# A three-layer float32 block on one core: the order on the engines comes from the scheduler's other machine model

## The chip, the core and the metric

The kernel runs on one core of a Trainium2 chip. The core has engines that each work through a queue of their own, in the order in which the queue was filled: TensorE (PE, matrix products; its weight loads are shown apart as PEld), VectorE (DVE), ScalarE (ACT), GpSimd (POOL) and SyncE (SP, which here only starts transfers). An instruction whose inputs are not there holds everything behind it on its own engine. The metric is the device time of one execution in microseconds (us), lower is better; the median over runs counts.

## What is computed

The reference is two blocks, one after the other, in float32, on 512 tokens of width 1024. Cut to what matters here:

```
# first block: 16 meta tokens are put ahead of the 512
h = h + 0.5 * swiglu(rmsnorm(h, norm_ffn1), w_ffn1_in, w_ffn1_out)
u = rmsnorm(h, norm_mix)
...                                   # u @ w_in -> fox attention, 16 heads; retention, 4 heads
mixed = g_a * (y_a @ w_o_fox) + g_b * (y_b @ w_o_ret)
h = h + mixed @ w_out
h = h + 0.5 * swiglu(rmsnorm(h, norm_ffn2), w_ffn2_in, w_ffn2_out)

# second block, two layers; the first of them also carries 256 context tokens on
h = modulate(x, sh1, sc1)             # layer_norm(x) * (1 + scale) + shift
y = ...                               # neighbourhood attention, spatial gating, grouped-query attention, @ w_o
x = layer_norm(ALPHA * x + g1 * y) * ln1_g[l] + ln1_b[l]
x = layer_norm(ALPHA * x + g2 * swiglu_2(modulate(x, sh2, sc2), ...)) * ln2_g[l] + ln2_b[l]
```

## The kernel before, in words

Activations lie transposed: eight tiles of 128 channels, tokens along the free axis, worked on in two halves of 256, 272 or 384 tokens. A product with a weight matrix runs in units of 128 output channels. Each unit's weights come from HBM by a transfer on SP's queue (`raw`), ACT rounds them to the high part (`whi`, line 269), DVE or POOL takes the rest (`wlo`, line 271), and `mm3` issues three products for each of the eight channel tiles: high by high (line 300), low activation (line 301), low weight (line 303). With eight tiles a unit is 24 matmuls on each half of the tokens. Three `whi`/`wlo` pairs and three `raw` tiles are in rotation, so the split of a later unit waits until an earlier unit's matmuls are done.

Between products stand norms. A layer norm of one half (`ln`) is a chain over four engines, and `postln` followed by `modulate` is two such chains, one behind the other:

1. POOL adds the tiles in pairs (line 1157), PE takes the mean over channels of the sums by a product with a constant matrix (line 1163, four matmuls), which leaves the mean in a PSUM tile;
2. DVE subtracts the mean from each of eight tiles (line 1168), ACT squares (line 1169), POOL adds the squares (line 441);
3. PE sums the squares over channels with single-column products (line 369); DVE makes the reciprocal root in ten small steps (lines 376, 333 to 353) and a diagonal matrix of it, `dg` (line 394);
4. PE spreads `dg` over all partitions (line 407); `postln` then scales on DVE and shifts on ACT (lines 1205, 1206), `modulate` writes the activations of the next product, high part on ACT (`ah`, line 1194) and low part on DVE (`al`, lines 1191, 1195).

The program is written by generators: a phase's products are written out, and the norm of the other half is advanced a step at a time between units. Three PSUM pools hold the results: `mm` for units, `at` for statistics, means, spreads and some units.

`run` wraps the program in a manual schedule for POOL, so POOL's queue keeps the order in which the program is written. The queues of PE, DVE, ACT and SP are filled by the framework's scheduler. It reads the whole program, plays it on a model of the machine, and where several instructions could go next on an engine it places the one that the model has ready; the program's order decides among those ready. Which model plays is an argument of the tile context. `_trace` opens two contexts: a dry one, whose only product is the list of weight units, and the real one.

Of the kernel before, what the change touches and what calls it, by code (L numbers as in the profile page):

```python
# [2069 lines left out]
def _trace(nc, I, out):  # L2070

    import concourse.bacc as bacc

    dry = bacc.Bacc("TRN2", target_bir_lowering=False, num_devices=1)
    J = {k: dry.dram_tensor("in_" + k, v.shape, F32, kind="ExternalInput").ap() for k, v in I.items()}
    o = dry.dram_tensor("out", out.shape, F32, kind="ExternalOutput").ap()
    plan = None
    try:
        with tile.TileContext(dry) as tc, ExitStack() as ctx:
            k = Kern(ctx, tc, J, o)  # L2080
            k.run()
            plan = k.plan
            raise _Dry
    except _Dry:
        pass
    with tile.TileContext(nc) as tc, ExitStack() as ctx:
        Kern(ctx, tc, I, out, plan).run()


# [12 lines left out]
```

## Time and profile before

| | |
|---|---|
| runs | 3388.63, 3375.97, 3386.22 us; median 3386.22 |
| the profiled execution | 3384.84 us |
| its span | 3383.0 us, so 1.84 us lie around the span |
| PE busy | 3220.5 us, 95% of the span, 19680 matmuls |
| DVE busy | 2088.1 us, 62% |
| ACT busy | 1320.8 us, 39% |
| POOL busy | 531.9 us, 16% |
| mean granted clock of PE | 0.978 of full speed |

PE is the engine that is nearly always busy. What is not PE's work is the idle time before a PE instruction, and each view of the waits names the step that ended it. A granted clock of 1.00 is 2.4 GHz and of 0.50 is 1.2 GHz.

### The profile page before, as it was taken

Reading aid. Unit: us, or ns where it says so; the run is one execution under the profiler, and the core shown is the slowest. Engines: PE = TensorE matmul, PEld = TensorE weight load, DVE = VectorE, ACT = ScalarE, POOL = GpSimd, SP = SyncE. Lnnn points to the kernel's source line nnn. Section 1 sums busy time; section 2 is a strip of 40 time slices with the busy share of each in tenths; the row PEclk is TensorE's granted clock in tenths of the full one; section 3 lists DMA queues with packets and bytes.
Section 4 is the critical chain, followed back from the end, with each engine's and each line's share of the span. In section 5 each row is a group of like instructions: output and inputs, shape, how many; then the busy total and the mean of one; then the engine's idle time right before and its main releaser. Section 6 shows DMA issues by size and latency. Waiting matters only on the chain. (4 is left out here: it accounts for less than half of the span.)

```text
span 3383.0 us, 50315 instructions
## 1 busy us (share of the span) xinstructions
PE 3220.5 (95%) x19680; PEld 2874.1 (85%) x19680; DVE 2088.1 (62%) x4433; ACT 1320.8 (39%) x2266; POOL 531.9 (16%) x500
## 2 busy tenths in 40 slices
PE   8999999999999999999898989999999999889998
PEld 8999979988888987889777878888898787888887
DVE  7994568876633769856676764222257586773335
ACT  4222346653323523234464543111135365552223
POOL 2000122333200100012212240000013212320001
PEclk9999999999999999999999999999999799999999
DMA  6663431122233556644001322221234201333233
GB/s 209 209 206 103 124 97 45 51 68 69 65 96 101 194 175 196 211 122 143 19 28 53 92 75 90 65 65 57 69 117 137 74 24 57 118 125 112 88 98 107
DMA packets 112461, 351.22 MB, mean 104 GB/s; under 512 B 12960, under 2 KB 26912, under 8 KB 111968
## 3 DMA queue, kind: packets, MB, share of 16 engines
q1 hardware_dynamic: 86464, 280.07, 26.8%
q10 hardware_dynamic: 25472, 65.84, 6.1%
q8 instruction: 155, 2.54, 0.3%
q0 software_dynamic: 288, 2.10, 0.2%
q14 instruction: 82, 0.67, 0.1%
HBM read 339.57 MB, written 8.39 MB: 103 GB/s over the span
## 5 line engine op out<-in xcount | busy, mean ns | idle before, releaser
L269 ACT ACTIVATE whi<-raw 128x1024 fp32r<-128x1024 f32 (+3 forms) x543 | 549.3, 1012 | 1413.8 <-PE mm L301 757.3
L300 PE MATMUL mm<-ah,whi 128*128 128x512 f32 (+3 forms) x2496 | 811.4, 331 | 11.9 <-ACT s L576 5.4
L301 PE MATMUL mm<-al,whi 128*128 128x512 f32 (+3 forms) x2496 | 787.5, 327 | 1.0 <-DVE al L1195 1.0
L271 DVE TENSOR_TENSOR wlo<-raw,whi 128x1024 fp32r<-128x1024 f32 (+2 forms) x464 | 559.5, 1208 | 328.7 <-ACT whi L269 324.6
L303 PE MATMUL mm<-ah,wlo 128*128 128x512 f32 (+3 forms) x2496 | 717.1, 328 | 5.5 <-DVE wlo L271 5.5
L300 PEld LDWEIGHTS mm<-ah,whi 128*128 128x128 f32 x2496 | 476.1, 191 | 65.2 <-ACT ah L1194 7.4
L301 PEld LDWEIGHTS mm<-al,whi 128*128 128x128 f32 x2496 | 475.8, 191 | 41.4 <-DVE al L1195 3.3
L300 PE MATMUL at<-ah,whi 128*128 128x512 f32 (+4 forms) x1368 | 479.5, 352 | 8.3 <-DVE B L1482 2.6
L301 PE MATMUL at<-al,whi 128*128 128x512 f32 (+4 forms) x1368 | 459.5, 337 | 0.1
L303 PEld LDWEIGHTS mm<-ah,wlo 128*128 128x128 f32 x2496 | 430.4, 191 | 32.9 <-DVE wlo L271 6.5
L303 PE MATMUL at<-ah,wlo 128*128 128x512 f32 (+4 forms) x1368 | 457.6, 336 | 0.0
L300 PE MATMUL mm<-gh,whi 128*128 128x256 f32 (+3 forms) x1168 | 377.0, 327 | 0.7 <-ACT gh L322 0.3
L301 PE MATMUL mm<-gl,whi 128*128 128x256 f32 (+3 forms) x1168 | 366.8, 323 | 0.7 <-DVE gl L323 0.7
L303 PE MATMUL mm<-gh,wlo 128*128 128x256 f32 (+3 forms) x1168 | 339.3, 324 | 0.3 <-DVE wlo L271 0.3
L300 PEld LDWEIGHTS at<-ah,whi 128*128 128x128 f32 x1368 | 265.6, 195 | 34.0 <-issue 5.3
L301 PEld LDWEIGHTS at<-al,whi 128*128 128x128 f32 x1368 | 266.4, 195 | 23.6 <-issue 3.3
L303 PEld LDWEIGHTS at<-ah,wlo 128*128 128x128 f32 x1368 | 265.5, 194 | 21.3 <-issue 0.5
L1157 POOL TENSOR_TENSOR sq<-x,x 128x256 f32<-128x256 f32 (+1 forms) x68 | 73.2, 1088 | 1211.2 <-DVE x L1214 815.1
L300 PEld LDWEIGHTS mm<-gh,whi 128*128 128x128 f32 x1168 | 220.6, 189 | 23.1 <-ACT gh L322 0.5
L301 PEld LDWEIGHTS mm<-gl,whi 128*128 128x128 f32 x1168 | 220.8, 189 | 17.9 <-DVE gl L323 1.4
L271 POOL TENSOR_TENSOR wlo<-raw,whi 128x1024 fp32r<-128x1024 f32 (+1 forms) x79 | 181.5, 2305 | 316.4 <-ACT whi L269 316.2
L582 DVE TENSOR_TENSOR s<-s,mm 128x256 f32<-128x256 f32 (+3 forms) x142 | 71.9, 525 | 233.7 <-PE mm L303 232.8
(403 smaller groups left out, 4839.4 us busy)
## 6 DMA issues: line engine op xcount, KB each, us to landing
raw<-in_wfin SPq DMA_DIRECT2D x116, 512.0 KB, 3.5
raw<-in_win SPq DMA_DIRECT2D x115, 512.0 KB, 3.6
wm<-in_wmod ACTq DMA_DIRECT2D x96, 512.0 KB, 4.2
raw<-in_w2in SPq DMA_DIRECT2D x52, 512.0 KB, 4.4
raw<-in_w1in SPq DMA_DIRECT2D x50, 512.0 KB, 3.7
raw<-in_wfout SPq DMA_DIRECT2D x48, 448.0 KB, 3.3
raw<-in_w1out SPq DMA_DIRECT2D x24, 448.0 KB, 3.4
raw<-in_w2out SPq DMA_DIRECT2D x24, 448.0 KB, 3.3
```

The lines of the kernel that those rows point to most:

```text
L269: self.nc.scalar.activation(hi, raw, AF.Copy)
L271: eng.tensor_tensor(lo, raw, hi.bitcast(F32), op=ALU.subtract)
L300: t.matmul(ps, wh, xh, start=start, stop=False)
L301: t.matmul(ps, wh, xl, start=False, stop=False)
L303: t.matmul(ps, wl, xh, start=False, stop=stop)
L582: nc.vector.tensor_tensor(s[:, c], s[:, c], ps[1][:, 512 * b:512 * b + n], op=ALU.mult)
L1157: nc.gpsimd.tensor_tensor(x, X[j][:, c], X[j + 1][:, c], op=ALU.add)
```

## The change

The real tile context is opened with an argument that selects the scheduler's other machine model, one that follows queues and semaphores. Nothing else differs: the program is written by the same code, and each engine gets the same instructions.

```
--- before.py
+++ after.py
@@ -2083,7 +2083,7 @@
             raise _Dry
     except _Dry:
         pass
-    with tile.TileContext(nc) as tc, ExitStack() as ctx:
+    with tile.TileContext(nc, schedule_with_timeline_sim=True) as tc, ExitStack() as ctx:
         Kern(ctx, tc, I, out, plan).run()
```

What moves: POOL's order is the same, by the manual schedule. On SP 16 transfers move, by at most four places. On PE 7586 of 19079 instructions stand elsewhere (mean 3.5 places, the farthest 124 earlier and 91 later), on ACT 1290, on DVE a similar share, by at most 25 places. Three places follow; in a row stand line, operation, output<-inputs with buffer numbers, and shape of the output.

**Place 1**, end of the second norm pair of the second block's first layer, around 2605 to 2621 us. `at_24789` is the PSUM tile of the first chain (`postln`), `at_25018` the mean of the second (`modulate`), `at_25038` the last product unit that is ready there. PE before and after, one piece of the difference:

```order
-L1163 MATMUL at_25018<-sq_25045,avg 128x384
 L300 MATMUL at_25038<-ah_24313,whi_24977 128x384
 L301 MATMUL at_25038<-al_24314,whi_24977 128x384
...
 L301 MATMUL at_25038<-al_24318,whi_24977 128x384
 L303 MATMUL at_25038<-ah_24317,wlo_24978 128x384
+L407 MATMUL at_24789<-dg_24967,ones 128x384
+L1163 MATMUL at_25018<-sq_25019,avg 128x384
+L1163 MATMUL at_25018<-sq_25024,avg 128x384
+L1163 MATMUL at_25018<-sq_25029,avg 128x384
+L1163 MATMUL at_25018<-sq_25045,avg 128x384
 L369 MATMUL at_25069<-ones,sq_25070 128x1 x3
```

The spread L407 stood ahead of the 24 products of the unit before `at_25038` (48 places earlier), and the four mean products stood between triples of `at_25038`. Now all five stand behind the unit's last product, and the next statistics follow at once. On DVE, at the same place:

```order
 L394 TENSOR_TENSOR dg_24967<-c_ident,rsy_24941 128x384
+L271 TENSOR_TENSOR wlo_25075<-raw_24981,whi_25074 128x1024
 L1205 SCALAR_TENSOR_TENSOR x_19019<-x_19019,c_cols,at_24789 128x384
...
 L1205 SCALAR_TENSOR_TENSOR x_19479<-x_19479,c_cols,at_24789 128x384
-L271 TENSOR_TENSOR wlo_25033<-raw_24933,whi_25032 128x1024
-L271 TENSOR_TENSOR wlo_25075<-raw_24981,whi_25074 128x1024
+L271 TENSOR_TENSOR wlo_25222<-raw_25036,whi_25221 128x1024
 L1168 TENSOR_TENSOR x_19019<-x_19019,at_25018 128x384
```

Two weight splits stood between the eight scalings (L1205) and the eight subtractions (L1168); both now stand ahead of the scalings (`wlo_25033` further up, ahead of the root's ten steps), and a later one takes their place.

**Place 2**, the first norm pair of the same layer, around 2016 to 2048 us. `at_20426` is the second chain's mean and spread, `at_20460` its statistics, `mm_20678` the last unit on the ready half, `mm_20712` and `mm_20745` the first units on the half that this chain makes. PE, one piece of the difference:

```order
 L301 MATMUL mm_20678<-al_19018,whi_20611 128x384
 L303 MATMUL mm_20678<-ah_19017,wlo_20612 128x384
+L1163 MATMUL at_20426<-sq_20427,avg 128x384
+L1163 MATMUL at_20426<-sq_20432,avg 128x384
+L1163 MATMUL at_20426<-sq_20437,avg 128x384
+L1163 MATMUL at_20426<-sq_20442,avg 128x384
+L369 MATMUL at_20460<-ones,sq_20461 128x1 x3
+L369 MATMUL at_20460<-ones,sq_20495 128x1 x3
+L407 MATMUL at_20426<-dg_20565,ones 128x384
 L300 MATMUL mm_20712<-ah_19003,whi_20672 128x384
+L300 MATMUL mm_20745<-ah_19003,whi_20706 128x384
```

The means moved back by 75 to 81 places, the statistics by 52 and 36, the spread by 19. No product unit is left between them. The first chain's spread (`at_20244`, not in the rows) moved back by 72, to 27 products ahead of the means.

**Place 3**, a norm of the first block, around 1140 us: `sq_12130` is a sum of squares that POOL makes, `mm_12119` and `mm_12160` product units that are ready. PE, one piece of the difference:

```order
 L301 MATMUL mm_12119<-al_11730,whi_12041 128x256
-L300 MATMUL mm_12160<-ah_11729,whi_12113 128x256
-L301 MATMUL mm_12160<-al_11730,whi_12113 128x256
-L369 MATMUL at_12129<-ones,sq_12130 128x1 x2
 L303 MATMUL mm_12119<-ah_11729,wlo_12042 128x256
...
 L301 MATMUL mm_12160<-al_11744,whi_12113 128x256
 L303 MATMUL mm_12160<-ah_11743,wlo_12114 128x256
+L369 MATMUL at_12129<-ones,sq_12130 128x1 x2
 L300 MATMUL mm_12205<-ah_11729,whi_12154 128x256
```

The statistics stood behind the first products of the two units; now both units stand ahead of them, 44 places.

## Rows read from the trace of the kernel before

**Rows 1.** Waits of PE over the span: total us, times, longest us.
```profile
PE at L369 <- POOL sq L441: 36.3, 22, 4.2
PE at L407 <- DVE dg L394: 27.3, 13, 4.1
```

**Rows 2.** Windows: length, busy us (count) of PE, PEld, DVE, ACT, POOL; granted clock, DMA share, GB/s.
```profile
400.00:490.00 90.00, 81.02 (x570) 72.77 (x569) 62.61 (x161) 37.32 (x69) 17.76 (x19) 0.92 0.39 119
...
1900.00:2000.00 100.00, 88.64 (x452) 78.00 (x450) 72.38 (x140) 41.43 (x69) 37.82 (x48) 0.97 0.30 93
2000.00:2060.00 60.00, 50.94 (x231) 45.11 (x232) 41.36 (x88) 29.89 (x57) 19.69 (x16) 0.86 0.24 73
...
2975.00:3030.00 55.00, 49.68 (x378) 46.79 (x377) 42.11 (x90) 32.73 (x63) 18.09 (x20) 1.00 0.38 119
...
sum 3383.00, PE 3220.55 PEld 2874.09 DVE 2088.08 ACT 1320.80 POOL 531.89; mean PE 161.03 PEld 143.70 DVE 104.40 ACT 66.04 POOL 26.59
```

**Rows 3.** Timeline of PE, 1130 to 1180 us: start, length, instruction, [idle before <-releaser].
```profile
1140.88 0.61 PE L369 MATMUL at<-ones,sq 128*128 128x1 f32 x4 [3.93 <-POOL sq L441]
```

**Rows 4.** Timeline of PE, 1640 to 1660 us.
```profile
1647.29 2.07 PE L1752 MATMUL at<-q,pm 128*128 128x512 f32 x2 [5.62 <-DVE q L1748]
```

**Rows 5.** Timeline of PE, 2600 to 2660 us.
```profile
2600.56 0.83 PE L369 MATMUL at<-ones,sq 128*128 128x1 f32 x6 [0.55 <-POOL sq L441]
...
2605.57 0.81 PE L407 MATMUL at<-dg,ones 128*128 128x384 f32 x2
...
2614.98 0.81 PE L1163 MATMUL at<-sq,avg 128*128 128x384 f32 x2
...
2617.02 0.34 PE L303 MATMUL at<-ah,wlo 128*128 128x384 f32 x1
2621.56 1.44 PE L369 MATMUL at<-ones,sq 128*128 128x1 f32 x6 [4.21 <-POOL sq L441]
2625.82 1.44 PE L369 MATMUL at<-ones,sq 128*128 128x1 f32 x6 [2.82 <-POOL sq L441]
2629.69 1.65 PE L407 MATMUL at<-dg,ones 128*128 128x384 f32 x2 [2.42 <-DVE dg L394]
2632.78 1.01 PE L300 MATMUL at<-ah,whi 128*128 128x384 f32 x2 [1.45 <-ACT ah L1194]
```

**Rows 6.** Timeline of POOL, 2595 to 2640 us.
```profile
2608.28 3.12 POOL L1157 TENSOR_TENSOR sq<-x,x 128x384 f32<-128x384 f32 x3 [7.77 <-ACT x L1206]
2612.61 1.87 POOL L1157 TENSOR_TENSOR sq<-x,x 128x384 f32<-128x384 f32 x1 [1.21 <-ACT x L1206]
```

**Rows 7.** Timeline of DVE, 2600 to 2640 us.
```profile
2610.62 3.00 DVE L271 TENSOR_TENSOR wlo<-raw,whi 128x1024 fp32r<-128x1024 f32 x2
```

**Rows 8.** Timeline of PE, 1999 to 2050 us.
```profile
2001.02 0.44 PE L300 MATMUL mm<-ah,whi 128*128 128x384 f32 x1 [2.25 <-ACT s L576]
...
2016.37 0.88 PE L407 MATMUL at<-dg,ones 128*128 128x384 f32 x2
...
2024.83 0.91 PE L1163 MATMUL at<-sq,avg 128*128 128x384 f32 x2 [0.63 <-POOL sq L1157]
```

**Rows 9.** Windows in which the granted clock was at its lower level.
```profile
438.30:445.10 6.80, 6.80 (x33) 6.80 (x33) 2.70 (x10) 1.34 (x2) 0.73 (x1) 0.50 0.28 87
...
1947.00:1950.40 3.40, 3.40 (x13) 3.40 (x12) 1.14 (x1) 0.70 (x2) 2.58 (x3) 0.50 0.48 146
2001.60:2011.80 10.20, 8.12 (x29) 7.62 (x28) 4.08 (x3) 3.54 (x7) 7.01 (x5) 0.50 0.33 103
2032.40:2039.20 6.80, 6.80 (x26) 6.80 (x25) 1.78 (x2) 2.70 (x5) 3.56 (x3) 0.50 0.36 116
2619.40:2636.50 17.10, 8.25 (x25) 6.67 (x26) 8.42 (x28) 6.98 (x14) 5.65 (x6) 0.50 0.29 101
2646.80:2667.30 20.50, 20.50 (x92) 19.56 (x92) 4.71 (x11) 5.68 (x9) 4.71 (x2) 0.50 0.38 121
2964.20:2974.40 10.20, 6.00 (x22) 5.05 (x23) 6.72 (x23) 2.62 (x6) 0.67 (x1) 0.50 0.14 49
```

More of the change, by code (lines that the diff above doesn't have):

```diff
@@ L2085, in _trace @@
         pass
-    with tile.TileContext(nc) as tc, ExitStack() as ctx:
+    with tile.TileContext(nc, schedule_with_timeline_sim=True) as tc, ExitStack() as ctx:
         Kern(ctx, tc, I, out, plan).run()
```

## The prediction

> **What bounds the kernel now.** I read the sum of busy times first. PE works 3220.55 us of a span of 3383.0 [rows 2], so 162.45 us of idle PE are all that any order can win in waiting. The matmuls themselves are the same before and after, and where nothing interrupts them they follow each other without a gap, so I take no gain from PE's work at full clock. Second, the waits of PE: the largest two groups are both norm steps, the statistics L369 waiting for POOL's sums of squares, 36.3 us in 22 waits, and the spread L407 waiting for DVE's diagonal, 27.3 us in 13 [rows 1]. Third, the windows: idle time is concentrated where one phase hands its result to the next through a norm, for example 9.0 us in 400 to 490, 11.4 in 1900 to 2000, 9.1 in 2000 to 2060 [rows 2]. Fourth, the granted clock: after a cluster of waits PE runs some us at its lower level, 0.50 [rows 9], so a wait costs twice, once idle and once slow.
>
> In the timeline the reader is to see two kinds of wait. At 1140.88 PE stands 3.93 us before a statistic though ready product units are behind it in the queue [rows 3]: an order can cover that. At 2621.56 to 2632.78 PE waits four times, 4.21, 2.82, 2.42 and 1.45 us, 10.9 in sum, and after 2617.02 no product is left that doesn't need the chain's result [rows 5]: there an order can only start the chain sooner or later.
>
> **What the change does.** Same instructions, POOL's order untouched, so every term is a wait that is covered, opened or moved. The new order treats both kinds alike: it postpones norm steps behind products. I cost each place by this rule: latency of the step's input by the rows, less the PE work that now stands between it and what started it, and no less than zero.
>
> *Waits that get covered.* Place 3: 3.93 us [rows 3] with two whole product units ahead instead of their beginnings; with 1 more for the products that waited behind it, 5. 400 to 490: 9.0 idle [rows 2], the statistic, the masked scores and their first weights all get products ahead of them; I take 8.5. 1900 to 2000: 11.4 idle in a dozen waits; most statistics and means move back behind units, I take 7. At 1647.29 a 5.62 us wait for DVE [rows 4] gets sixteen matmuls ahead of it; eight of 512 or 256 columns and eight products are about 3 us, so 3. Elsewhere: the windows of rows 2, the 3.9, the 5.6 and place 1's 10.9 hold 55 of the 162 us; the other hundred are mostly small waits in attention, group norms and first units. For these I bound from both sides: 0, if the new places are no better than the old, and 35, if a third goes. Near the lower end, because the group norms' spreads come out with as much cover as before by the order; I take 11. Sum 34.5.
>
> *Norm steps that end up at the end of a phase.* Place 1: L407 at 2605.57 waits for nothing today; 48 products stand between it and the last product at 2617.02 [rows 5]. Moved behind them, with the statistic that feeds it, it starts where those products end. Today that is 2617.36 (2617.02 + 0.34), less the five norm products that leave the stretch (about 0.4 each of the engine's time, 2.0) and less the wait of 0.55 at 2600.56 that vanishes: 2614.8, that is 9.2 later. From L407 to the last mean product at 2614.98 the chain took 9.4 us, and POOL's last sum ended at 2614.48 (2612.61 + 1.87) [rows 6], half a us before that product, so the chain has no slack in it and everything to 2632.78 shifts: 9.2, less what place 1 of DVE gives back. The two weight splits that stood between scalings and subtractions, 3.00 us [rows 7], leave the chain; beside them POOL's sum took 1.87 where three others took 3.12, 1.04 each [rows 6]. So 0.8 comes back, and with slack elsewhere I take +8.
>
> The Trainium skill, SBUF — State Buffer, Who interferes with whom and its summary, says that a DVE operation with two SBUF inputs and a GpSimd operation that reads SBUF shut each other out, and the one that issues second waits for the whole of the first. The 1.87 agrees with that. By this rule the gain here is the 0.8 that the row gives, but wherever a split now lands beside a sum of squares it would take the same from the chain; it moves the sum by about a us either way.
>
> Place 2: the chain from L407 at 2016.37 to the last mean at 2024.83 takes 8.5 us [rows 8]; behind the new L407 stand 27 products of 384 columns, 5.1 us at about 0.19 (48 of them with five norm products took 11.5 [rows 5]), so 3.4 open. From the last mean on nothing covers. The same stretch in rows 5, 2614.98 to 2632.78, took 17.8, of which 10.9 idle and 2.4 still covered by products; without these 13.3. Together 16.7 idle. Today's window has 9.1 [rows 2], of which the 2.25 at 2001.02 [rows 8] stays, so 6.8 goes: +10.
>
> The last layer's first norm pair, around 2947 to 2971, has the same 48-place move of its L407 as place 1, with 256 columns in place of 384: two thirds of 9.2 is 6.1, +6. In 2975 to 3030 there are 5.3 idle [rows 2]; two statistics move 84 and 66 places, to stand with the spread straight ahead of the first product on the half that they make. Idle by the intervals in rows 5, between the statistics 2.8, to the spread 2.4, to the first product 1.5, and 3.5 before the first of them (between 0 and the 4.21 there), is 10.2: +5. Three more places, around 447, 1270 and 1523, have a spread or statistic that comes out short of cover but with products behind it; rows 1 give 1.65 and 2.1 us as the mean of such waits, a step waits on two, and I take 3 each: +9. Sum 38.
>
> *Clock.* Six short stretches at 0.50 follow waits that get covered, the first at 438.30 and the last at 1947.00 [rows 9], 3.4 or 6.8 us each, 30.6 in all; nearly all of it is work that would take half, so 14.5 come back. The stall at 2621 drew 8.25 + 20.50 us of work at 0.50, 14.4 lost. The three tails that grow to its size (2016, 2947, 3006) I put at 9 each, since the stall must be whole to draw all of it: 27, less the 7.5 and 3 that the first two lose today (half of 8.12 + 6.80, and of 6.00 [rows 9]). That is 16.5, net +2.
>
> Sum: -34.5 + 38 + 2 = +5.5. On the profiled execution's 3384.84 that is 3390.3; the median of the runs is 1.4 above that execution, so I forecast 3392 for the median.
>
> **The rivals.**
> *The new order is simply better (faster).* A queue model that knows who is late would place a step where its input really arrives, and then the tails must not grow. For it: the covered waits are certain by the order, and the small ones could give 35 in place of 11. Against it: L407 at 2605.57 waits for nothing today and still goes back. If the postponed steps' chains find DVE, ACT and POOL free and shorten by half, the 38 become 19, the clock gives back 10 in place of costing 2, and small waits give 25: -48.5 + 19 - 10 = -39.5, so 3347. It decides from the point where the chain from L407 to the first product of the next phase takes under 20 us at place 1, against 27.2 (2605.57 to 2632.78) today.
>
> *The splits pulled ahead hold the norms (slower).* On DVE, splits that depend on a transfer and on ACT's rounding now stand ahead of the root and the scalings. DVE waits in order, so a split whose `whi` isn't there holds the norm behind it, and PE's end of phase with it. Seventeen layer norms of a half could meet it. The price is bounded by 0, if each `whi` is there, and by two splits of 1.5 us [rows 7] at each, 51. At half, 25, added to 5.5: 3417. For it: the rotation of three pairs frees a split's tile only when PE has finished a unit, close to the time at which the norm step is due. Against it: at place 1 the unit that frees `wlo_25033`'s tile ends before L407's old place, so its split can lie under products. It decides from a DVE wait of over 1 us for ACT's `whi` ahead of a root in most halves.
>
> *Nothing to be seen.* Most of PE's 7586 moved instructions are products that swap with products, at a mean of 3.5 places. If the covers cancel within each phase, the result lies within 5 us of today's.
>
> **How the numbers follow.** I give my forecast, a small loss of covers against tails, 0.36; the order that hides itself 0.08; the better order 0.25; the held norms or tails at their full price 0.31. What a measurement of this kernel can tell from no change is about 0.5%, 17 us. Faster by more than that takes the better order: 0.25. Slower by more takes held norms, or tails and clock both at the top: 0.31. The rest, 0.44, lies between. The range reaches to the better order and past the held norms: 3348 to 3424. For the likeliest case alone it is 3374 to 3408, from small waits at 25 to clock and tails each 8 dearer.
>
> **What would show it.** Right: the 3.93 at 1140 gone, with no slow clock after it; PE idle around 2016 to 2050 up from 6.8 to some 17, in one row of waits for L1163, L369, L407 and the first `ah`; at place 1 L407 with nothing but norm steps behind it and the first product of the next layer some 8 us later after the last unit than today's 15.4 (2617.36 to 2632.78). PE's total idle would stay near 166. Wrong: total idle under 140, or the tails no longer than before, which would say that the postponed steps had slack that these rows don't show; or DVE waiting for `whi` ahead of the roots.

## The result and the profile after

The changed kernel takes 3459.95 us in the median of four runs (3455.33 to 3465.96), the kernel before 3385.09 beside it: a ratio of 1.0232 [1.0218, 1.0246], 75 us slower. The forecast of 3392 is wrong, and its range ends 36 us below.

The page's first part and the waits of PE over the span, after (total us, times, longest):

```profile
PE 3244.2 (94%) x19680; PEld 2906.0 (84%) x19680; DVE 2089.5 (60%) x4433; ACT 1317.9 (38%) x2266; POOL 534.7 (15%) x500
```
```profile
PE at L369 <- POOL sq L441: 41.7, 16, 5.8
PE at L407 <- DVE dg L394: 31.0, 12, 5.1
PE at L1163 <- POOL sq L1157: 14.9, 9, 3.1
PE mm L300 <- ACT s L576: 9.2, 8, 2.1
PE at L1360 <- DVE pl L323: 8.4, 14, 1.1
```

The profiled execution took 3465.96 us with a span of 3463.9, 80.9 more than before [rows 2]. PE's idle time went from 162.45 to 3463.9 - 3244.2 = 219.7, that is +57.2; its busy time went from 3220.5 to 3244.2, +23.7, for the same 19680 matmuls, at a mean granted clock of 0.962 against 0.978. Against [rows 1] the two large waits became fewer (22 to 16, 13 to 12) and longer in sum. The new order makes waits deeper, and only these two kinds fewer: over the span PE stood idle for more than 0.15 us 162 times before and 167 times after, for more than 1 us 44 and 73 times, for more than 3 us 6 and 17 times.

The stretches of [rows 2] after, each with nearly the same PE work (columns as there):

```profile
389.00:479.30 90.30, 79.09 (x568) 69.61 (x567) 60.93 (x161) 37.41 (x68) 17.72 (x19) 0.94 0.38 118
1920.00:2035.20 115.20, 95.80 (x474) 88.22 (x473) 71.31 (x136) 43.27 (x71) 34.97 (x47) 0.90 0.26 80
2035.20:2097.40 62.20, 47.13 (x231) 42.55 (x231) 42.68 (x92) 29.47 (x57) 20.17 (x16) 0.84 0.21 68
...
3045.50:3107.00 61.50, 51.04 (x371) 48.78 (x371) 44.61 (x89) 32.55 (x62) 20.13 (x20) 0.89 0.33 104
```

Idle of PE is length less its busy time: 9.0 became 11.2 at 400, 11.4 became 19.4 at 1900, 9.1 became 15.1 at 2000, 5.3 became 10.5 at 2975. In none of them does PE stand less than before.

To see where the time went I took, for a time t of the trace of before, the number of PE instructions that had started by t, and compared the time at which the same number had started in another kernel. The growth of that difference from one t to the next is what a stage lost. Steps of 2 to 4 us also appear between equal orders, as in start_new, which behind 300 us has the orders of before; there they add up to +11 from 400 us on, so a column's sum over many stages is no better known than that. For after and for the experiments below (us; "to" is in the time of before):

```
  to     after start_new fox_spend fox_hold tails_new norm_new norm_old hold_all
  400    -11.0    -9.5     +1.0     -9.3     -2.7     +8.6     -0.8     -7.4
  490     +0.3    -1.5     -3.6     +0.8     +0.5     -0.7     -1.4     -4.1
  750    +16.1    +0.1    +15.5     +7.0     +0.1     -0.0    +16.1    +14.6
  930     +8.4    +4.5     -0.8     +6.9     +3.9     +8.3     +4.6     +6.1
 1200     +1.0    +2.2     +2.1     +1.2     +0.4     +2.8     -0.4     +0.1
 1930    +10.5    +0.3     -3.9     +7.2     -4.3     +4.5    +15.2     +3.1
 2060    +12.1    -0.1     -2.3     +8.9     +0.7     +8.6    +12.7     +1.3
 2580     +0.3    +3.8     -0.1     +3.0     +2.8     -1.2     +1.5     +2.1
 2645    +13.2    -0.4     -0.4    +13.8    +13.9    +14.4     +2.0     +0.7
 2940    +16.4    +1.1     +1.0    +16.6     +6.5     +9.7     +5.8     -1.5
 3035    +10.6    +1.1     +1.1    +10.3     +9.4     +8.3     +7.4     +2.6
 3380     +2.8    -0.0     -0.2     +2.8     +1.9     +2.1     +3.0     +1.2
```

The ends of phases that the forecast named (to 2060, 2645, 3035) lose 36 us. The first stage gains 11. The rest, some 55 us, lies in stages of which the forecast expected little, most of it gains.

**Place 1 after.** PE from the last product of the phase to the first of the next, answering [rows 5], and DVE beside it, answering [rows 7]:

```profile
2657.51 0.34 PE L303 MATMUL at<-ah,wlo 128*128 128x384 f32 x1
2657.68 0.81 PE L407 MATMUL at<-dg,ones 128*128 128x384 f32 x2
2661.45 0.91 PE L1163 MATMUL at<-sq,avg 128*128 128x384 f32 x2 [2.96 <-POOL sq L1157]
...
2665.48 0.91 PE L1163 MATMUL at<-sq,avg 128*128 128x384 f32 x2 [1.02 <-POOL sq L1157]
2671.35 1.44 PE L369 MATMUL at<-ones,sq 128*128 128x1 f32 x6 [4.95 <-POOL sq L441]
2675.60 1.44 PE L369 MATMUL at<-ones,sq 128*128 128x1 f32 x6 [2.81 <-POOL sq L441]
2679.46 1.65 PE L407 MATMUL at<-dg,ones 128*128 128x384 f32 x2 [2.42 <-DVE dg L394]
2682.56 1.01 PE L300 MATMUL at<-ah,whi 128*128 128x384 f32 x2 [1.45 <-ACT ah L1194]
```
```profile
2654.09 0.56 DVE L394 TENSOR_TENSOR dg<-c_ident,rsy 128x384 f32<-128x384 f32 x1
...
2658.53 4.29 DVE L1205 SCALAR_TENSOR_TENSOR x<-x,c_cols,at 128x384 f32<-128x384 f32 x8 [2.73 <-PE at L407]
2662.74 1.84 DVE L271 TENSOR_TENSOR wlo<-raw,whi 128x1024 fp32r<-128x1024 f32 x1
2666.43 3.81 DVE L1168 TENSOR_TENSOR x<-x,at 128x384 f32<-128x384 f32 x8 [1.85 <-PE at L1163]
```

The diagonal is done at 2654.65 (2654.09 + 0.56); the spread that needs it starts at 2657.68, 3.0 us later, because 17 products stand between in PE's queue. Until it starts DVE waits 2.73 us for it, and PE waits for all that follows. From the end of the last product to the first of the next layer it takes 24.7 us, where before it took 15.4.

**All norms.** Worked out over the two traces: for each norm step on PE the time from the end of its last input from another engine to its own start.

```
                 before: mean  median   sum     after: mean  median   sum
spread L407 (37)         0.48   0.06     18            1.50   0.75     55
statistic L369 (204)     1.77   0.50    361            2.89   2.34    589
```

Half of the spreads started within 0.06 us of their input before, within 0.75 after. Of the 55 us ahead of the spreads after, PE spent some 52 on products, of the 589 ahead of the statistics about 400; the rest is mostly other norm steps and other work of PE. In that time the norm's chain, four engines long, stands still.

### The profile page after: what moved, and what is told of

Same layout as the page of the kernel before. It is cut to its first block, busy times and chain, and to the rows that moved or that the text cites. A ratio compares the mean times of both kernels' runs of the same rounds, so it can differ in the third digit from the quotient of the medians.

```text
span 3463.9 us, 50424 instructions
## 1 busy us (share of the span) xinstructions
PE 3244.2 (94%) x19680; PEld 2906.0 (84%) x19680; DVE 2089.5 (60%) x4433; ACT 1317.9 (38%) x2266; POOL 534.7 (15%) x500
## 4 chain that ended last, share of the span: by engine, by line
PE 81%; DVE 8%; issue 4%; ACT 4%; POOL 2%; DMA 1%; ACTq 0%; POOLq 0%; DVEq 0%
PE mm L300 17%; PE mm L303 17%; PE mm L301 17%; PE at L300 7%; PE at L301 6%; PE at L303 6%; PE at L1360 2%; PE at L369 1%; PE at L1368 1%; POOL sq L441 1%; ACT whi L269 1%; DVE wlo L271 1%; PE at L1163 1%; PE at L407 1%; PE at L1377 1%
## 5 line engine op out<-in xcount | busy, mean ns | idle before, releaser
L303 PE MATMUL at<-ah,wlo 128*128 128x512 f32 (+4 forms) x1368 | 466.7, 342 | 0.5 <-DVE wlo L271 0.3
L300 PEld LDWEIGHTS at<-ah,whi 128*128 128x128 f32 x1368 | 272.7, 200 | 47.3 <-ACT ah L322 5.4
L301 PEld LDWEIGHTS mm<-gl,whi 128*128 128x128 f32 x1168 | 219.7, 188 | 17.0
L303 PEld LDWEIGHTS mm<-gh,wlo 128*128 128x128 f32 x1168 | 202.4, 188 | 10.9
```

The costliest lines, as they stand in the source:

```text
L300: t.matmul(ps, wh, xh, start=start, stop=False)
L301: t.matmul(ps, wh, xl, start=False, stop=False)
L303: t.matmul(ps, wl, xh, start=False, stop=stop)
```

## The experiments

All kernels schedule the program twice in dry passes, once by each model (`old`, `new`), and then force pieces of one of the orders on the real pass by pairs "b not before a" of instructions of one engine. `_of(order, eng, "PE")` is the row of one engine. Such a pair adds no semaphore and no wait between engines.

```
+    old, new_ = ordered(False), ordered(True)
...
+        for a, b in _edges(old, new_, eng, fn):
+            tc.add_manual_dep(L[b], L[a].name,
+                              mybir.DependencyInfo(mybir.DependencyClass.NoSync, mybir.DependencyReason.DATA),
```

**pe_new, rest_new, pe_old, rest_old: one engine's order alone.** The first two force after's order on PE, or on DVE and ACT, and let the model of before choose the rest; the last two are their mirrors.

```
+    return {"PE": _of(new, eng, "PE")}                                # pe_new; old: pe_old
+    return {e: _of(new, eng, e) for e in ("DVE", "Activation")}       # rest_new; old: rest_old
```

> Here PE's order is that of the kernel after, word for word; the order on DVE, ACT and SP is chosen anew by the model of the kernel before, for this PE order. Theory P (the loss is made in PE's queue: products stand ahead of steps that the other engines wait for) expects most of the 75 us, 3430 to 3465. Rival D (it is made on DVE and ACT, where weight splits stand ahead of norm and attention steps) expects little of it, 3380 to 3405.

> Here DVE's and ACT's orders are those of the kernel after, word for word; PE's and SP's are chosen anew by the model of the kernel before, within what these two allow. Theory P expects 3380 to 3405, rival D 3430 to 3465. About 3420 to 3425 would say that the two share it.

> PE's order is that of the kernel before, word for word; DVE's, ACT's and SP's orders are chosen by the new model for this PE order. Theory F expects 3385 to 3405. If the new model's orders on DVE and ACT (weight splits ahead of norm steps) cost by themselves, rival D, 3415 or more; as pe_new and rest_new lay far above both kernels, orders of two models that do not fit each other may cost as much here, 3450 to 3520.

> DVE's and ACT's orders are those of the kernel before, word for word; PE's and SP's are chosen by the new model within them. If a postponed PE step costs only through a queue of DVE or ACT that is built around it, 3385 to 3405; if PE's own order makes the loss, 3430 to 3465; orders that do not fit each other, above 3480.

Measured: pe_new 3512.76 us, 1.0365 [1.0341, 1.0389]; rest_new 3594.39, 1.0610 [1.0588, 1.0631]; pe_old 3432.74, 1.0140 [1.0120, 1.0160]; rest_old 3559.25, 1.0521 [1.0502, 1.0540]. Three of the four are slower than both kernels. An order on one engine and an order on another that were made by different models don't fit each other, and the misfit (up to 6%) is larger than what was asked. pe_old lies between the two kernels, where rival D had been put (3415 or more) and not where a misfit had been (3450 to 3520), so by its time alone rival D stands. Their times don't split the change, and I draw no share from them; single stages of them do tell something, at the end of this section. DVE's queue is no bystander in the change: 3114 of its 4433 instructions stand elsewhere in after, up to 51 places earlier and not by at most 25, a larger share than on PE.

**norm_new and norm_old: the norm steps of PE alone.** norm_new is the kernel before with each norm step held behind the product behind which it stands in after; norm_old is after with them held ahead of the products ahead of which they stand in before.

```
+NORM = ("Kern.tokstat", "Kern.bcasting", "Kern.ln")
+    for k, x in enumerate(n):                       # n: PE's row of after, at: places in before
+        if fn[x] in NORM and fn[n[k - 1]] not in NORM and k:
+            last = n[k - 1]
+        if fn[x] in NORM and last is not None and at[last] > at[x]:
+            out.append((last, x))
```

> The kernel before, with one thing moved: each norm step on PE (statistics, means, spreads) that the change puts further back may not start before the product behind which it stands after the change. Theory N (the postponed norm steps are the whole loss) expects 3440 to 3465. The prediction's own terms for them, +38 less what covered waits give back, expect 3395 to 3425. If the loss is in the attention stages, 3380 to 3395.

> The kernel after, with the norm steps on PE held ahead of the product ahead of which they stand before the change. Theory N expects 3380 to 3400. If attention has a loss of its own of about half, 3415 to 3435; if the norm steps cost nothing, 3455 to 3465.

Measured: norm_new 3448.96, 1.0183 [1.0167, 1.0200]; norm_old 3452.26, 1.0196 [1.0179, 1.0212]. Postponing the norm steps is enough to lose 62 us, but taking it back in after returns only about 12 (1.0232 to 1.0196): it gives back place 1 (+13.2 to +2.0) and 10.6 in the stage to 2940, and not place 2 (+12.7). The norm steps are one way to lose the time and not the whole of it. Nor are norm_new's 62 us the same loss as after's: +8.6 of them lie ahead of 400 us, where after gains 11, and none in the stage to 750, where after loses 16. norm_old in turn gives up the gain of the first stage (-0.8).

**tails_new: norm_new's pairs at the three named phase ends only** (1960 to 2060, 2530 to 2645, 2940 to 3035 us of before).

```
+WHERE = [(11661, 12020), (14691, 15189), (16859, 17410)]
-        if fn[x] in NORM and last is not None and at[last] > at[x]:
+        if fn[x] in NORM and last is not None and at[last] > at[x] and any(a <= at[x] < b for a, b in WHERE):
```

> The kernel before, with the postponed norm steps of norm_new at three places only, the norm pairs between phases of the second block (around 1960 to 2060, 2530 to 2645 and 2940 to 3035 us). The prediction put 10 + 8 + 6 + 5 = 29 us on them plus up to 16 of clock, so 3414 to 3430. From norm_new's own stages, +9, +14 and +8, 3414 to 3418. Under 3400 if it needs the changed order elsewhere.

Measured: 3412.49, 1.0067 [1.0042, 1.0091], just under both expected ranges; by stage +13.9 at place 1, +9.4 from 2940 to 3035, +6.5 behind place 1, but +0.7 at place 2. So postponing norm steps at place 1 and at the last layer's norms makes what after loses there (+13.2, +10.6). At place 2 it doesn't by itself; norm_new, which also postpones the norm steps ahead of it, has +8.6 there.

**start_new and fox_new: whole pieces of after's orders.** On PE, DVE, ACT and SP alike, after's orders up to PE's place 2200 (300 us) and before's behind it, and after's orders only from 300 to 1060 us, the attention of the first block and what follows.

```
+NEW = [(0, 2200)]        # fox_new: [(2181, 6774)]
+    for x in old:
+        part[x] = any(a <= pe < b for a, b in NEW)
+        pe += eng[x] == "PE"
```

> The orders of the kernel after up to 300 us of the program (2181 to 2200 PE instructions), in the middle of the first feed-forward products; from there on the orders of the kernel before, on PE, DVE, ACT and SP. The stage table of the first two traces has the kernel after 9 to 10 us ahead at that point. If that lead belongs to the order of the first stage alone, 3373 to 3378, faster than both kernels; if it is a debt that is paid back later, 3383 to 3388.

> The orders of the kernel after only between 300 and 1060 us of the program (first attention, retention, output products of the first block), both ends in plain product stretches; elsewhere those of the kernel before. The stage table has the kernel after lose 23 to 24 us there. If the losses are local, 3406 to 3412; if a queue carries them on, above 3420; if the region's loss is only what the first stage's lead cost, 3383 to 3395.

Measured: start_new, in five rounds, 3379.44 against 3390.87, 0.9974 [0.9959, 0.9989]; fox_new, in three, 3410.0, 1.0060 [1.0038, 1.0082]. start_new's time lies between its two expected ranges, on a chip on which before takes 3390.87 where it took 3385.09 beside after; measured against that, start_new beats both kernels, the one before by 0.26%, some 9 us, so the gain of the first stage stays. This rests on the medians alone: in the one trace of start_new the lead of 9.5 is used up by the steps between equal orders, and it ends 1.5 us behind the trace of before. fox_new's loss is local as expected: its trace has +15.8 in the stage to 750 and +8.3 to 930, where after has +16.1 and +8.4, and +4 in the sum of the eight stages behind. The windows of 0 to 60 and 60 to 300 us, before and start_new:

```profile
0.00:60.00 60.00, 47.20 (x296) 45.12 (x297) 42.45 (x107) 30.59 (x57) 18.44 (x32) 0.94 0.60 202
60.00:300.00 240.00, 236.75 (x1918) 234.54 (x1918) 205.72 (x499) 60.23 (x81) 16.01 (x12) 0.99 0.60 191
```
```profile
0.00:60.00 60.00, 50.67 (x324) 49.29 (x325) 39.82 (x96) 31.80 (x58) 18.80 (x32) 0.97 0.59 197
60.00:300.00 240.00, 238.97 (x1969) 238.77 (x1969) 215.17 (x516) 61.90 (x84) 18.26 (x13) 1.00 0.62 196
```

PE's idle went from 12.8 to 9.3 us and from 3.3 to 1.0, 5.7 in sum; the rest of the lead of 9.5 goes with the clock, 0.94 to 0.97 and 0.99 to 1.00 (an estimate: 0.03 x 60 + 0.01 x 240 = 4.2 us).

**fox_spend and fox_hold: products ahead of attention.** fox_new moves the rows of four engines; these two ask whether pairs on PE alone, and only between products and attention, make the loss. In fox_spend they move 241 instructions of PE, and the model moves 96 of DVE and 52 of ACT with them, all but four between 690 and 750 us. In after PE works off product units earlier and the attention steps later. fox_spend is the kernel before with the attention steps of 690 to 745 us held behind the products behind which they stand in after; fox_hold is after with the products of that stretch held behind the attention steps behind which they stand before.

```
+WHERE = (4866, 5136)                                    # fox_spend
+        if fn[x] == "Kern.mm3":
+            last = x
+        elif WHERE[0] <= at[x] < WHERE[1] and last is not None and at[last] > at[x]:
+            out.append((last, x))
+HELD = (4866, 5136)                                     # fox_hold
+        if fn[x] != "Kern.mm3":
+            last = x
+        elif HELD[0] <= k < HELD[1] and last is not None and at[last] > at[x]:
+            out.append((last, x))
```

> The kernel after, with the product units of the last stretch of the first attention (270 PE places, 690 to 745 us) held behind the attention steps behind which they stand before the change, so that they are left as cover. Theory F (products that were spent early are missing as cover when the attention's last chain and POOL's first weight split run alone) expects 8 to 15 us less than the kernel after, 3445 to 3452. If the attention's chain itself is late because of DVE's or ACT's order, 3456 to 3462.

> The mirror of fox_hold: the kernel before, where in the last stretch of the first attention (270 PE places, 690 to 745 us) each attention step may not start before the product behind which it stands after the change. Nothing else is told to move. Theory F expects the loss that fox_hold took away from the kernel after, 6 to 12 us, in the stages from 690 to 760 us, so 3390 to 3397; if the loss there needs the changed order of DVE and ACT or the earlier stages, 3382 to 3387.

Measured: fox_spend 3402.19, 1.0060 [1.0043, 1.0077], a larger loss than expected, with +15.5 in the stage to 750 where after has +16.1 (its trace is the fastest of its four executions and ends only 9.5 us behind before); fox_hold 3454.43, 1.0189 [1.0165, 1.0212], with +7.0 there, between its two expected ranges in time and by the ratio 14 us under after. Around the attention's end, first POOL and then PE in the timeline, for before, for after, and for fox_spend (there PE by its largest wait in 690 to 770):

```profile
741.37 0.55 POOL L988 MEMSET decm<- 128x512 f32 x1 [21.31 <-DVE ya L939]
...
742.39 7.58 POOL L271 TENSOR_TENSOR wlo<-raw,whi 128x1024 fp32r<-128x1024 f32 x3
```
```profile
744.20 0.40 PE L303 MATMUL mm<-ah,wlo 128*128 128x512 f32 x1
...
744.92 0.44 PE L303 MATMUL mm<-ah,wlo 128*128 128x272 f32 x2
```
```profile
745.24 0.55 POOL L988 MEMSET decm<- 128x512 f32 x1 [32.27 <-DVE ya L939]
...
746.25 7.46 POOL L271 TENSOR_TENSOR wlo<-raw,whi 128x1024 fp32r<-128x1024 f32 x3
```
```profile
743.38 0.33 PE L919 MATMUL at<-y,VT 128*128 128x128 f32 x1
748.65 0.81 PE L303 MATMUL mm<-ah,wlo 128*128 128x272 f32 x2 [4.94 <-POOL wlo L271]
```
```profile
752.56 0.55 POOL L988 MEMSET decm<- 128x512 f32 x1 [34.03 <-DVE ya L939]
...
753.58 7.45 POOL L271 TENSOR_TENSOR wlo<-raw,whi 128x1024 fp32r<-128x1024 f32 x3
```
```profile
PE mm L303 <- POOL wlo L271: 4.9, 1, 4.9
```

POOL keeps the program's order: its splits for the next phase stand behind memsets that wait for the last attention output (`ya`, L939). Before, products of 512 columns still ran while POOL made its first split (2.4 us a split), and the first product that needs it followed at 744.92 without a wait. In after that unit had been worked off earlier, and PE stands 4.94 us. The windows from 690 (684 in after) to 770, before, after, fox_spend:

```profile
690.00:770.00 80.00, 75.82 (x450) 63.97 (x449) 57.57 (x149) 40.31 (x84) 25.04 (x14) 1.00 0.25 78
```
```profile
684.00:770.00 86.00, 76.86 (x423) 64.50 (x422) 53.24 (x144) 39.16 (x84) 23.94 (x14) 0.90 0.21 65
```
```profile
690.00:770.00 80.00, 69.09 (x359) 56.83 (x359) 50.14 (x135) 35.43 (x75) 18.14 (x11) 0.89 0.19 57
```

Idle of 4.2 became 9.1 and 10.9, and the clock went from 1.00 to 0.90 and 0.89. (fox_spend's window holds fewer matmuls, since its loss lies in it.) Of fox_spend's 15.5 us the added idle time is 6.7, of which 4.94 is the wait for POOL; a granted clock of 0.89 over 80 us is an estimated 17.6 us at the lower level (0.11 x 2 x 80), and half of that, 8.8, is about the rest. Pairs that only let ready products go ahead of attention steps are enough to make this loss.

**hold_all: after with every product held** behind the last non-product step of PE behind which it stands before. The pairs are on PE alone; the rest of the order is the new model's choice under them.

```
+HELD = (0, 1000000)
```

> The kernel after, scheduled by its own model, with every product on PE held behind the last other step (norm or attention) behind which it stands before the change. DVE, ACT and the order among the products stay the new model's choice. Theory F (what costs is that products go ahead of steps which others wait for) expects nearly all of the loss gone, 3385 to 3405, or 10 less with the lead of the first stage. If DVE's and ACT's order has a cost of its own, 3415 to 3445.

Measured: 3396.46 against 3382.86, 1.0034 [1.0023, 1.0046]. Of the 75 us 61 are gone, the gain of the first stage stays (-7.4), place 2 is at +1.3, place 1 at +0.7, and the stage to 2940 at -1.5. Its waits of PE, and the windows over place 1 of hold_all, before and after:

```profile
PE at L369 <- POOL sq L441: 33.1, 16, 4.3
PE at L407 <- DVE dg L394: 26.7, 15, 4.1
```
```profile
2595.00:2660.00 65.00, 52.34 (x264) 46.85 (x262) 44.65 (x97) 32.27 (x58) 23.54 (x23) 0.87 0.34 111
```
```profile
2595.00:2660.00 65.00, 52.74 (x265) 48.26 (x264) 37.04 (x90) 31.58 (x57) 16.63 (x17) 0.77 0.30 98
```
```profile
2640.00:2705.00 65.00, 46.27 (x220) 40.73 (x218) 35.01 (x87) 28.40 (x53) 16.43 (x16) 0.79 0.27 89
```

Both waits are near [rows 1] again, and the window's idle of 12.7 us is near the 12.3 of before and below the 18.7 of after; the mean spread starts 0.54 us after its input (0.48 before, 1.50 after). DVE follows PE here: at place 1 its two splits stand between scalings and subtractions again, as in [rows 7]. So its DVE queue is not after's (2246 of 4433 places differ), and not that of before either (2676 differ). What remains of the loss lies in the attention's stages, +14.6 and +6.1. Of the 14.6 only 1.0 falls from 710 to 750, where after loses 13.6; the other 13.6 fall from 490 to 710, where after loses 2.5 and pe_old, with PE's queue of before, 12.8. So that part goes with the new model's orders on DVE and ACT around PE's old order, and is no part of after's loss.

**Two places through all the runs.** `L919` is the last attention product of the first block; the first column is its place in PE's queue, the third the number of products between place 1's first spread (L407) and the end of the unit, both counted in the kernels' queues. The losses are taken as in the table of stages; before has 5110 and 48.

```
            L919 at   710 to 750   behind L407   2580 to 2645
after        5134       +13.6            0          +13.2
pe_new       5134       +15.1            0          +14.2
rest_old     5134       +12.6            0           +6.7
rest_new     5134       +17.1           23          +15.4
fox_spend    5134       +13.4           48           -0.4
fox_new      5134       +13.5           48           -0.0
norm_old     5134       +13.7           48           +2.0
fox_hold     5110        +1.0            0          +13.8
norm_new     5110        +0.0            0          +14.4
tails_new    5110        +0.0            0          +13.9
start_new    5110        +0.0           48           -0.4
hold_all     5110        +1.0           48           +0.7
pe_old       5110        +0.2           48           +0.3
```

At both places the loss goes with PE's queue (rest_new has 23 products behind L407, but like the kernels with none it has no product left behind the last mean, where the others have nine). rest_old has the orders of before on DVE and ACT and loses; pe_old has the new model's orders there and doesn't. That rules rival D out at these two places, which are a third of the 81 us.

## Why the prediction was wrong

**What bounds the kernel** was right: the same matmuls, and all of the loss is PE's idle time (+57.2) and its longer busy time (+23.7, at a lower mean clock).

**The tails** held at place 1 and in the last layer, and nearly in sum. At place 1 the forecast was that L407 starts where the products end and everything to the first product shifts, +8; from the last product to the first of the next layer it is +9.3, and 13.2 with the waits just ahead. The chain from L407 to that product takes 24.9 us (27.2 before): shorter by 2.3 where 0.8 was taken, and far from the 20 at which the better order would have won. The mean products wait 2.96 and 1.02 us where they waited for nothing; tails_new shows the same stage from pairs on the norm steps alone. 2947 and 2975 together came out at +10.6 for 11; the three small ones, +9, are at most the 5.5 from 1500 to 1570, with +0.3 around 447 and -0.5 around 1270. Place 2 with the covers just ahead of it, +10 and -7, came out at +12.1:

```profile
2062.42 1.45 PE L1163 MATMUL at<-sq,avg 128*128 128x384 f32 x4
2064.87 0.91 PE L1163 MATMUL at<-sq,avg 128*128 128x384 f32 x2 [0.99 <-POOL sq L1157]
2066.80 0.91 PE L1163 MATMUL at<-sq,avg 128*128 128x384 f32 x2 [1.02 <-POOL sq L1157]
2072.67 1.44 PE L369 MATMUL at<-ones,sq 128*128 128x1 f32 x6 [4.95 <-POOL sq L441]
2076.92 1.44 PE L369 MATMUL at<-ones,sq 128*128 128x1 f32 x6 [2.81 <-POOL sq L441]
2080.78 1.65 PE L407 MATMUL at<-dg,ones 128*128 128x384 f32 x2 [2.42 <-DVE dg L394]
2083.88 1.01 PE L300 MATMUL mm<-ah,whi 128*128 128x384 f32 x2 [1.46 <-ACT ah L1194]
```

Its waits in a row are 13.7 us in PE's timeline of after, for the 16.7 expected; the covers ahead of it are what didn't come. All in all these stages lost 37.5 to 41.4 us, clock included, where 31 was forecast, or 47.5 with the 16.5 of clock that the forecast put on the tails. But at place 2 postponed norm steps by themselves make +0.7, so which moves make that one is open.

**The covers** gave nothing. The single waits did go: at place 3 there is no wait for L369 any more. The stage gave nothing: -5 forecast, +1.0 measured. After, in the same work, 1138.5 to 1214.8, by the window and by the largest wait of PE:

```profile
1138.50:1214.80 76.30, 70.90 (x525) 68.21 (x524) 61.92 (x135) 39.81 (x65) 4.97 (x7) 0.96 0.62 210
```
```profile
PE mm L300 <- ACT s L576: 3.3, 2, 2.1
```

5.4 us idle, for 6.1 in the same 525 matmuls before. Likewise -8.5 at 400 to 490 became +0.3, and -3 at 1647 became +3.8 from 1570 to 1670.

And the small covers, **"For these I bound from both sides: 0, if the new places are no better than the old, and 35, if a third goes"**, of which I took 11: this is the step that failed. It had no loss in it. The stages behind it, 0 to 400, 490 to 930, 1670 to 1930 and 2645 to 2940, measured -11.0 + 24.5 + 1.8 + 16.4 = +31.7, so 43 us off. The bound took a product worked off early as free. fox_spend shows at one place that it isn't: the products are what lay over the attention's last steps and POOL's split, and their absence costs 15.5 us there. In 2645 to 2940 no run follows the single step; holding the products takes the whole loss back (hold_all, -1.5), the norm steps alone about two thirds of it (norm_old, +5.8). In 750 to 930 (+8.4) and 1670 to 1930 the step stays open. Without the 7 ahead of place 2, the covers were forecast at -27.5 and came out at +36.8 (1.0 + 0.3 + 3.8 + 31.7, clock included): 64 of the 75 us between the forecast of +5.5 and the 80.6 by which after is behind at 3380 us. PE's total idle, which was to stay near 166, is 219.7.

**The clock**, +2, was sized from three tails and six covered waits. It became part of the 23.7 us of busy time, mostly elsewhere than forecast: the mean granted clock over place 1, 0.79 for 0.77 before, and over place 2, 0.84 for 0.86, hardly moved; it fell at the last norms, 0.89 for 1.00, as forecast, but also at the attention's end, 0.90 for 1.00, and ahead of place 2, 0.90 for 0.97, where the forecast had no loss. By the two traces' records of the clock PE was busy at the lower level for 115 us before and 201 after. At half speed the 86 us more are an estimated 43 lost, more than the 23.7 that appear; no run explains the difference.

**The rivals.** The better order was wrong, though it holds in the first 300 us. The held norms had the nearer time, 3417, by a mechanism that is not there: over the 37 norms the root starts 0.17 us after its last statistic in after (0.13 before), at most 1.0, and the diagonal is ready 4.11 us after it (4.20 before). The splits on DVE don't stand in the way of the roots, and at the two places followed through all the runs PE's queue does. The queue model also didn't hide itself by cancelling within a phase.

**How cause and effect are shown.** That the loss comes from products of PE's queue going ahead of steps for which other engines wait is shown at the attention's end and at place 1, in all thirteen kernels, whatever the orders on DVE and ACT. For the whole kernel it rests on hold_all (pairs on PE's products alone, 61 of 75 us back), in which DVE and ACT follow, so a share of their orders is not excluded elsewhere. Forward, fox_spend and tails_new lose in their own stages what after loses there, but for place 2. The shares don't add up: norm_new loses 62, norm_old regains 12. Not shown is why the model behind the argument places ready products first; no run looks into it.

## What to carry to other kernels

A ready product is a stock of cover that can be spent once. When an order moves it ahead, look for the step that it now delays and for the wait that it used to hide, and put a loss into the bound of every stage whose rows you don't follow. A norm step whose output three engines wait for should start when its input is there, products or not; count the time from input to start, not its waits on PE, which can fall in number while the kernel slows. Of a scheduler's order take the piece that a stage shows to be better, as the first 300 us here, and force the rest back.

## What the runs showed of the hardware

Waits cost twice over, more than I had sized: the same 19680 matmuls kept PE busy for 23.7 us more when 57 us of idle time were added in deeper gaps (6 of over 3 us before, 17 after). With only two clock levels, 1.2 and 2.4 GHz, a mean granted clock of 0.978 over 3383.0 us is an estimated 149 us at the lower one (0.022 x 2 x 3383.0), and 0.962 over 3463.9 us 263; the traces' records of the clock have 146 and 264, and no level but these two. start_new's 240 us at a granted clock of 1.00 show the other end: with 1.0 us idle the mean shows no slow stretch.
